# Value columns projected as token rows, keys scaled ahead of queries, and a freed tile for gates, in one hybrid transformer layer

## The chip, the cores and the metric

The kernel runs on one core of one Trainium2 chip. The metric is the device time of one execution in microseconds (us); lower is better. The engines are TensorE (PE; PEld is its weight load), VectorE (DVE), ScalarE (ACT), GpSimd (POOL) and SyncE (SP), which issues most DMAs.

## The reference

One layer on 2048 tokens of width 1024. Only the first of its three sub-layers is touched:

```python
IN_SIZES = (SWA_WIDTH, SWA_KV_WIDTH, SWA_KV_WIDTH,            # 512, 128, 128: window attention
            HGRN_WIDTH, HGRN_WIDTH, HGRN_WIDTH, HGRN_WIDTH)   # 4 x 512: q, f, i (the values), g (the gates)
...
def hgrn2(q, f_logit, i, g, lb, onorm_g):
    """f = lb + (1-lb) sigmoid(f_logit), k = 1-f,
    S_t = diag(f_t) S_{t-1} + k_t i_t^T,  o_t = S_t^T q_t,
    output = RMSNorm(o) * silu(g)."""
    ...
    A = jnp.einsum('bhnqd,bhnkd->bhnqk', qc * jnp.exp(b - b_mid), kc * jnp.exp(b_mid - b))
    A = jnp.where(causal, A, 0.0)
    o_intra = jnp.einsum('bhnqk,bhnkv->bhnqv', A, vc)
    kv = jnp.einsum('bhnkd,bhnkv->bhndv', kc * jnp.exp(b_last - b), vc)
    ...   # scan over chunks of 64: S = decay * S + kv
    o_inter = jnp.einsum('bhnqd,bhndv->bhnqv', qc * jnp.exp(b), S_prev)
    o = (o_intra + o_inter)
    o = rms_norm(o, onorm_g) * jax.nn.silu(g.astype(f32))
```

One input projection, u @ w_in, gives all of q, k, v of the window attention and q, f, i, g of the recurrence (4 heads of 128, chunks of 64 tokens). Behind both stand an output projection, cross attention into 256 memory tokens and a SwiGLU network.

## The kernel before

The sequence is worked in two halves of 1024 tokens. The first half's projection comes first (to about 240 us). Then `in_proj` projects the second half (to about 625 us) while the window attention (`swa_front`, `swa_back`) and recurrence of the first half and, later, the window attention of the second half run between its matmuls. The recurrence of the second half (`hgrn` over pairs 8 to 15; a pair is 128 tokens, two chunks) runs from about 625 to 745 us, between matmuls that fold cross-attention weights together (`fold_cross`, L170 to L172 and L131, L134). From about 765 us on come the big products (L1123 to L1125) to the end.

`in_proj` goes through 22 columns of 128 outputs in the order that `ORDER` lists: per head h the pair (10+h, 6+h), decay and query, then (14+2h, 15+2h); 14 to 17 are the values, 18 to 21 the gates. For a column, `in_cols` loads 1024 x 128 weights (`wcols`), splits them on POOL (L152, whi) and VectorE (L153, wlo), and multiplies them as the stationary operand with the split tokens u, 512 tokens at a time, 24 matmuls for each of two "g" banks (L684, L685, L687). A bank is emptied by ScalarE (L690, tanh, then L697 on VectorE for queries and gates; L704, a copy, for values). So z lies as features by tokens, and is stored to z_d with rows of 1024 tokens. A decay column goes on through `decays`, whose last step is L743 on VectorE. L1033 forms sums of weight tiles for the later products, on VectorE too.

In the recurrence, pair n loads k (`k1`), q (`qq`, `q1`), v and later the gates (`sg`), 512 features by 128 tokens each, from z_d. `hgrn_front`: POOL scales half of q (L868, into qq), TensorE forms the masked products (L878), POOL makes q6 (L884) and scales k (L887), TensorE transposes k and v (L890, L895), ScalarE copies them out (kt at L892, vt at L897). `hgrn_state` updates W from kt and vt (L907, L911 on POOL, L912 on VectorE). `hgrn_out` forms the output from vt, at, W and q6 (L922, L924), with a mean square through POOL (L930 h_vv, L932 h_rs). In the program's names a number ends the tile's own: k18 is k1 of pair 8, q68 is q6 of pair 8, k114 is k1 of pair 14.

The order of the instructions on each engine is not written by hand: the framework schedules the whole program against a simulated timeline, under the limits of the tile rings. io tiles (z, u) have 2 buffers, split weights and raw weights 3, v, kt and sg 1, qq, k1, q6 and vt 2.

Of the kernel before, what the change touches and what calls it, by code (L numbers as in the profile page):

```python
# [23 lines left out]
DFF = 2816  # L24
KT = D // P
NFF = DFF // P
NB = 2
TB = T // NB
NPB = TB // P
# [4 lines left out]
C_KA, C_VA, C_QH, C_FH, C_IH, C_GH = 512, 640, 768, 1280, 1792, 2304  # L34
# [14 lines left out]
class Layer:  # L49
# [125 lines left out]
    def run(self):  # L175
        tc, nc, I = self.tc, self.nc, self.I
        self._n = 0
        kw = dict(reuse_waits="tile")
        self.z_d = tc.dram_tile([DIN, T], F32, name="z_d")
        self.y_d = tc.dram_tile([NT, P, KT, P], F32, name="y_d")  # L180
        self.h1t_d = tc.dram_tile([NT, P, KT, P], F32, name="h1t_d")
        self.pt_d = tc.dram_tile([NT, P, KT, P], F32, name="pt_d")
        self.h1_d = tc.dram_tile([T, D], F32, name="h1_d")
        self.h2_d = tc.dram_tile([T, D], F32, name="h2_d")
        self.qk_d = tc.dram_tile([D, D], F32, name="qk_d")
        self.vo_d = tc.dram_tile([D, D], F32, name="vo_d")
        self.u_d = tc.dram_tile([KT, P, T], F32, name="u_d")
        self.h_d = tc.dram_tile([NFF, P, T], F32, name="hid_d")
        self.y2_d = tc.dram_tile([T, D], F32, name="y2_d")
        with (  # L190
            tc.tile_pool(name="cst", bufs=1) as self.cst,
            tc.tile_pool(name="sm", bufs=3, **kw) as self.sm,
            tc.tile_pool(name="edge", bufs=1, side="right") as edge,
        ):
            self.consts()

            for pool in (self.cst, edge):
                nc.gpsimd.memset(pool.tile([P, 24], F32, name="pad"), 0.0)
# [466 lines left out]
    def in_proj(self, b, u):  # L665
        order = [c for p in self.ORDER for c in p]
        e1 = None
        for cols in [order[:2]] + [[c] for c in order[2:]]:
            e1 = self.in_cols(b, u, cols, e1)
            yield  # L670

    def in_cols(self, b, u, cols, e1):
        nc = self.nc
        w = []
        for c in cols:
            w.append(self.wcols(self.I["w_in"], c))
        z = [self.io_tile("z") for _ in cols]
        for s in range(TB // 512):
            sl = slice(s * 512, (s + 1) * 512)
            for i, c in enumerate(cols):  # L680
                c0 = c * P
                ps = self.bank("g")
                for k in range(KT):
                    nc.tensor.matmul(ps, w[i][0][:, k, :], u[s][k][0], start=(k == 0), stop=False)  # L684
                    nc.tensor.matmul(ps, w[i][0][:, k, :], u[s][k][1], start=False, stop=False)  # L685
                for k in range(KT):
                    nc.tensor.matmul(ps, w[i][1][:, k, :], u[s][k][0], start=False, stop=(k == KT - 1))  # L687
                zs = z[i][:, sl]
                if c0 < C_QH or C_IH <= c0 < C_GH:
                    nc.scalar.activation(zs, ps, AF.Copy)  # L690
                else:
                    nc.scalar.activation(zs, ps, AF.Tanh, scale=0.5)
                    if C_FH <= c0 < C_IH:
                        h = (c0 - C_FH) // P
                        nc.gpsimd.tensor_scalar(zs, zs, self.fb[:, h:h + 1], self.fa[:, h:h + 1], ALU.mult, ALU.add)
                    else:
                        nc.vector.scalar_tensor_tensor(zs, zs, 1.0, ps, ALU.add, ALU.mult)  # L697
# [148 lines left out]
    def hgrn_front(self, n, kinds, f):  # L846
        nc, ph = self.nc, self.hg
        t0 = n * P
        z = self.z_d
        kinds = itertools.cycle(kinds)  # L850

        def get(t, c):
            self.load(t, z[c:c + 512, t0:t0 + P].rearrange("(h p) t -> p h t", p=P))
            return t

        def new(tag, bufs=1, w=P):
            return ph.tile([P, 4, w], F32, tag=tag, name=f"{tag}{n}", bufs=bufs)
# [4 lines left out]
        k1 = get(new("k1", 2), C_FH)  # L862
        qq = new("qq", 2, 192)
        q1 = get(qq[:, :, 0:P], C_QH)
        v = get(new("v"), C_IH)
        g1 = self.G1[:, n, :].unsqueeze(2).broadcast_to([P, 4, 64])

        nc.gpsimd.tensor_tensor(qq[:, :, P:192], qq[:, :, 64:P], g1, ALU.mult)  # L868

        at = self.atz[n % 2]  # L870
        if n < 2:
# [2 lines left out]
        for i in range(2):  # L874
            ps = self.bank(next(kinds))[:, 0:384].rearrange("p (h t) -> p h t", h=2)
            hs = slice(2 * i, 2 * i + 2)
            for r in range(2):
# [2 lines left out]
            nc.scalar.activation(at[0:64, hs, 64:P], ps[0:64, :, P:192], AF.Copy)  # L880

        yield
        q6 = new("q6", 2)
        nc.gpsimd.tensor_tensor(q6.rearrange("p h (c t) -> p h c t", t=64), q1.rearrange("p h (c t) -> p h c t", t=64),  # L884
                                self.G[:, n, :, :].unsqueeze(3).broadcast_to([P, 4, 2, 64]), ALU.mult)

        nc.gpsimd.tensor_tensor(k1[:, :, 0:64], k1[:, :, 0:64], g1, ALU.mult)  # L887
        ps = self.bank(next(kinds))
        for h in range(4):
            nc.tensor.transpose(ps[:, h * P:(h + 1) * P], k1[:, h, :], self.ident)  # L890
        kt = new("kt")
        nc.scalar.activation(kt, ps.rearrange("p (h t) -> p h t", h=4), AF.Copy)  # L892
        ps = self.bank(next(kinds))
        for h in range(4):
            nc.tensor.transpose(ps[:, h * P:(h + 1) * P], v[:, h, :], self.ident)  # L895
# [892 lines left out]
```

## Time and profile before

| | |
|---|---|
| time, median of 3 runs | 2548.94 us (2548.52 to 2550.93) |
| profiled execution | 2549.81 us, span 2548.1 us |
| mean granted TensorE clock | 0.997 |
| TensorE busy | 2508.5 us, 12004 matmul records |
| VectorE, ScalarE, POOL busy | 1761.2, 1250.5, 461.8 us |

In a timeline row stand start, duration, engine, line, operation, output and inputs by the program's names without numbers, stationary and moving shape, and, in brackets, the idle time before it and what ended that. Matmuls overlap, so the distance of their starts is the pace, not the duration. A group row gives the same for all instructions of a kind: count, then busy time and mean ns, then idle time before them.

### The profile page before, as it was taken

To read this page: it belongs to the slowest core of one execution; us is meant where nothing else is said; L and a number is where in the kernel's file an instruction comes from. 1 tells how busy PE (TensorE), PEld (TensorE's weight loads), DVE (VectorE), ACT (ScalarE), POOL (GpSimd) and SP (SyncE) were. 2 spreads that over 40 slices of the span, in tenths; PEclk is the share of its full clock that TensorE was granted. 3 is DMA by queue.
4 is the path that set the end of the run, shared out by engine and by line. 5 is a ranking of instruction groups with operands and counts; after the bars stand their busy time and mean duration, and the time that the engine had idled before them with its cause. 6 is when DMAs were issued, how large, how long until landed. Compare 5 with 4: busy or idle time off the path is not lost. (4 is left out here: it accounts for less than half of the span.)

```text
span 2548.1 us, 34095 instructions
## 1 busy us (share of the span) xinstructions
PE 2508.5 (98%) x12004; PEld 2090.5 (82%) x12004; DVE 1761.2 (69%) x2813; ACT 1250.5 (49%) x2606; POOL 461.8 (18%) x641
## 2 busy tenths in 40 slices
PE   8999999999999999999999999999999999999998
PEld 7777888878998878888788888888888888888886
DVE  6869587788767587787875655586566566664756
ACT  5454366556655566565554333353333344543543
POOL 2233233223412243233210000000000000000022
PEclk9999999999999999999999999999999999999999
DMA  6263544566987795859974542254555433666798
GB/s 240 96 218 137 175 140 139 165 202 209 296 303 223 210 279 196 280 187 253 302 229 133 175 147 79 95 182 144 182 195 194 161 128 132 205 209 195 223 226 207
DMA packets 269386, 489.97 MB, mean 192 GB/s; under 512 B 20640, under 2 KB 127136, under 8 KB 268704
## 3 DMA queue, kind: packets, MB, share of 16 engines
q1 hardware_dynamic: 255392, 438.52, 51.1%
q0 software_dynamic: 12672, 46.14, 9.0%
q10 hardware_dynamic: 1152, 3.15, 0.3%
q8 instruction: 94, 1.54, 0.3%
q14 instruction: 76, 0.62, 0.1%
HBM read 326.26 MB, written 161.48 MB: 191 GB/s over the span
## 5 line engine op out<-in xcount | busy, mean ns | idle before, releaser
L1123 PE MATMUL psm<-T,S 128*128 128x512 f32 x2744 | 1063.5, 392 | 9.5 <-ACT S L986 4.9
L1124 PE MATMUL psm<-T,S 128*128 128x512 f32 x2744 | 1070.8, 390 | 0.0
L1125 PE MATMUL psm<-T,S 128*128 128x512 f32 x2744 | 1063.9, 391 | 3.0 <-DVE S L989 2.5
L1123 PEld LDWEIGHTS psm<-T,S 128*128 128x128 f32 x2744 | 516.0, 188 | 121.6 <-ACT S L986 6.2
L1125 PEld LDWEIGHTS psm<-T,S 128*128 128x128 f32 x2744 | 515.7, 188 | 114.8 <-DVE S L989 7.4
L1124 PEld LDWEIGHTS psm<-T,S 128*128 128x128 f32 x2744 | 516.0, 188 | 106.5
L986 ACT ACTIVATE S<-sum 128x512 fp32r<-128x512 f32 (+1 forms) x336 | 205.9, 618 | 328.5 <-PE psm L1125 325.5
L989 DVE TENSOR_TENSOR S<-sraw,S 128x512 fp32r<-128x512 f32 (+1 forms) x312 | 211.0, 683 | 214.9 <-ACT S L986 193.8
L989 DVE TENSOR_TENSOR S<-sum,S 128x512 fp32r<-128x512 f32 (+1 forms) x400 | 271.9, 685 | 77.8 <-ACT S L986 61.9
L1138 ACT ACTIVATE part<-psm 128x512 f32<-128x512 f32 x294 | 173.2, 592 | 184.4 <-PE psm L1125 183.1
L986 ACT ACTIVATE S<-sraw 128x512 fp32r<-128x512 f32 (+1 forms) x271 | 165.9, 617 | 161.9 <-PE psm L1125 149.5
L1495 POOL DMA_DIRECT2D row<-y_d x28 | 25.0, 891 | 1071.3 <-DMA sraw<-hid_d 905.3
L1466 ACT ACTIVATE junk<-row 128x512 f32<-128x512 f32 x160 | 99.6, 625 | 96.1 <-DVE row L1488 32.6
L684 PE MATMUL psg<-u,whi 128*128 128x512 f32 x352 | 142.5, 405 | 3.7 <-DVE z L697 2.2
L989 DVE TENSOR_TENSOR T<-row,T 128x1024 fp32r<-128x1024 f32 x104 | 124.3, 1202 | 31.7 <-ACT T L986 31.5
L685 PE MATMUL psg<-u,whi 128*128 128x512 f32 x352 | 142.5, 405 | 0.0
L986 ACT ACTIVATE T<-row 128x1024 fp32r<-128x1024 f32 x104 | 105.3, 1023 | 23.3 <-DMA row<-in_w_down_dram 9.8
L687 PE MATMUL psg<-u,wlo 128*128 128x512 f32 x352 | 96.0, 402 | 0.7 <-DVE wlo L153 0.7
L153 DVE TENSOR_TENSOR wlo<-raw,whi 128x1024 fp32r<-128x1024 f32 x54 | 68.3, 1269 | 39.0 <-ACT whi L150 16.4
L1670 DVE TENSOR_TENSOR part<-psm,part 128x512 f32<-128x512 f32 x66 | 45.5, 689 | 63.8 <-PE psm L1125 63.5
L1661 DVE TENSOR_TENSOR row<-psm,part 128x512 f32<-128x512 f32 x66 | 45.5, 689 | 55.3 <-PE psm L1125 52.7
L988 POOL TENSOR_SCALAR S<-sum 128x512 fp32r<-128x512 f32 x64 | 50.8, 795 | 168.9 <-PE psm L1125 136.0
(343 smaller groups left out, 3462.8 us busy)
## 6 DMA issues: line engine op xcount, KB each, us to landing
sraw<-in_w_gate_dram SPq DMA_DIRECT2D x44, 512.0 KB, 5.0
sraw<-in_w_up_dram SPq DMA_DIRECT2D x44, 512.0 KB, 4.9
hid_d<-row SPq DMA_DIRECT2D x44, 512.0 KB, 2.8
h_d<-row SPq DMA_DIRECT2D x32, 512.0 KB, 7.0
y_d<-row SPq DMA_DIRECT2D x32, 512.0 KB, 3.6
sraw<-hid_d SPq DMA_DIRECT2D x32, 512.0 KB, 5.0
row<-h_d POOLq DMA_DIRECT2D x30, 512.0 KB, 7.7
row<-y_d POOLq DMA_DIRECT2D x28, 512.0 KB, 7.6
```

The costliest lines, as they stand in the source:

```text
L153: nc.vector.tensor_tensor(lo, raw, f32(hi), ALU.subtract)
L684: nc.tensor.matmul(ps, w[i][0][:, k, :], u[s][k][0], start=(k == 0), stop=False)
L685: nc.tensor.matmul(ps, w[i][0][:, k, :], u[s][k][1], start=False, stop=False)
L687: nc.tensor.matmul(ps, w[i][1][:, k, :], u[s][k][0], start=False, stop=(k == KT - 1))
L986: self.nc.scalar.activation(hi, raw, AF.Copy)
L988: self.nc.gpsimd.tensor_scalar(hi, raw, 1.0, 1.0, ALU.mult, ALU.mult)
L989: self.nc.vector.tensor_tensor(lo, raw, f32(hi), ALU.subtract)
L1123: nc.tensor.matmul(ps, s[:, 0, k, :], t[:, 0, k, :], start=st, stop=False, **kw)
L1124: nc.tensor.matmul(ps, s[:, 0, k, :], t[:, 1, k, :], start=False, stop=False, **kw)
L1125: nc.tensor.matmul(ps, s[:, 1, k, :], t[:, 0, k, :], start=False, stop=sp, **kw)
L1138: nc.scalar.activation(t, ps, AF.Copy)
L1466: self.nc.scalar.activation(junk, a, AF.Square, scale=float(D) ** -0.5, accum_out=to)
```

## The change

Three things are done for the second half only.

1. The value columns 14 to 17 are computed the other way round: tokens (128 of them) are the stationary operand and 256 value features the moving one (`value_cols`, `in_values`). w_in's value columns come as a host array `w_v` of four blocks, two of them (two raw tiles, two split pairs) for each half of the features. A bank holds two groups of 128 tokens by 256. The result goes to a new DRAM array v_d, tokens by 512 features. Pairs 8 to 15 load `vt` straight from it; their v tile, its four transposes and the copy fall away.
2. k is scaled before q6 is made, and for pairs 8 to 15 `issue_after` keeps q6 of a pair, and the scaled half of q of the next pair, behind the scaled k.
3. The gates of pairs 9, 11, 13, 15 take the buffer of tag "v", which no second-half pair uses now.

```diff
+        self.v_d = tc.dram_tile([TB, 512], F32, name="v_d")
...
         for cols in [order[:2]] + [[c] for c in order[2:]]:
-            e1 = self.in_cols(b, u, cols, e1)
+            c0 = cols[0] * P
+            if not C_IH <= c0 < C_GH:
+                e1 = self.in_cols(b, u, cols, e1)
+            else:
+                i, s = divmod(cols[0] - C_IH // P, 2)
+                if not s:
+                    w = self.value_cols(i)
+                self.in_values(i, s, u, w)
             yield
+
+    def value_cols(self, i):
+        w = []
+        for q in range(2):
+            raw = self.raw_tile()
+            self.load(raw, self.I["w_v"][2 * i + q])
+            hi, lo = self.split_tiles()
+            self.split(raw, hi, lo)
+            hi, lo = (t.rearrange("p (k c) -> p k c", c=256) for t in (hi, lo))
+            w += [(hi[:, k, :], lo[:, k, :]) for k in range(4)]
+        return w
+
+    def in_values(self, i, s, u, w):
+        nc = self.nc
+        z = self.io_tile("z")
+        for q in range(2):
+            ps = self.bank("g")
+            for j in range(2):
+                ts = slice((2 * q + j) * P, (2 * q + j + 1) * P)
+                pr = ps[:, j * 256:(j + 1) * 256]
+                for k in range(KT):
+                    nc.tensor.matmul(pr, u[s][k][0][:, ts], w[k][0], start=(k == 0), stop=False)
+                    nc.tensor.matmul(pr, u[s][k][1][:, ts], w[k][0], start=False, stop=False)
+                for k in range(KT):
+                    nc.tensor.matmul(pr, u[s][k][0][:, ts], w[k][1], start=False, stop=(k == KT - 1))
+            nc.scalar.activation(z[:, q * 512:(q + 1) * 512], ps, AF.Copy)
+        self.store(self.v_d[s * 512:(s + 1) * 512, i * 256:(i + 1) * 256].rearrange("(n p) c -> p n c", p=P),
+                   z.rearrange("p (n c) -> p n c", c=256))
...
-        v = get(new("v"), C_IH)
+        if n < NPB:
+            v = get(new("v"), C_IH)
+        else:
+            vt = new("vt", 2)
+            self.load(vt.rearrange("p h t -> p (h t)"), self.v_d[(n - NPB) * P:(n - NPB + 1) * P, :])
...
-        nc.gpsimd.tensor_tensor(qq[:, :, P:192], qq[:, :, 64:P], g1, ALU.mult)
+        with self.tc.issue_after(self.scaled) if n > NPB else contextlib.nullcontext():
+            nc.gpsimd.tensor_tensor(qq[:, :, P:192], qq[:, :, 64:P], g1, ALU.mult)
...
+        nc.gpsimd.tensor_tensor(k1[:, :, 0:64], k1[:, :, 0:64], g1, ALU.mult)
+        self.scaled = nc.cur_bb.bb.instructions[-1]
         q6 = new("q6", 2)
-        nc.gpsimd.tensor_tensor(q6.rearrange(...), q1.rearrange(...), self.G[...], ALU.mult)
-
-        nc.gpsimd.tensor_tensor(k1[:, :, 0:64], k1[:, :, 0:64], g1, ALU.mult)
+        with self.tc.issue_after(self.scaled) if n >= NPB else contextlib.nullcontext():
+            nc.gpsimd.tensor_tensor(q6.rearrange(...), q1.rearrange(...), self.G[...], ALU.mult)
...
-        ps = self.bank(next(kinds))
-        for h in range(4):
-            nc.tensor.transpose(ps[:, h * P:(h + 1) * P], v[:, h, :], self.ident)
-        vt = new("vt", 2)
-        nc.scalar.activation(vt, ps.rearrange("p (h t) -> p h t", h=4), AF.Copy)
+        if n < NPB:
+            ...   # the same five lines
...
-        sg = ph.tile([P, 4, P], F32, tag="sg", name=f"sg{n}")
+        sg = ph.tile([P, 4, P], F32, tag="v" if n > NPB and n % 2 else "sg", name=f"sg{n}")
...
+    w = np.asarray(inputs["w_in"]).reshape(D, DIN)
+    host["w_v"] = np.ascontiguousarray(w[:, C_IH:C_GH].reshape(2, 4, P, 2, 256).transpose(3, 0, 2, 1, 4)).reshape(4, P, D)
```

The scheduler then puts the instructions in another order from the first value column (about 395 us) to the end of the recurrence; outside of that stretch the order is the same. Lines behind the new functions have other numbers in the kernel after: L131 and L170 to L172 stay, L806 is L842 there, L868 L909, L878 L919, L884 L928, L887 L924, L890 L933, L907 L951, L911 L955, L922 L966, L924 L968, L697 L733, L743 L779, L799 L835, L1033 L1077. Three places follow.

TensorE at the start of the second half's recurrence, before (vt8 and v9 are the value tiles of pairs 8 and 9, L895 the transposes of v, L170 and L171 the folding):

```order
L895 MATMUL pst_855_6500<-ident_77,v8_6463 128x128 x4
L890 MATMUL psg_854_6493<-ident_77,k18_6459 128x128 x4
L878 MATMUL pst_864_6579<-qq9_6569,k19_6567 128x192 x2
L131 MATMUL psh_841_6407<-ident_77,u_836_6392 128x128 x4
L131 MATMUL psh_848_6431<-ident_77,u_843_6416 128x128 x4
L170 MATMUL pss_851_6446<-mT0_6388,whi_850_6442 128x256
L907 MATMUL psg_862_6560<-vt8_6505,kt8_6498 128x128 x4
L878 MATMUL psg_863_6574<-qq9_6569,k19_6567 128x192 x2
L895 MATMUL pst_868_6614<-ident_77,v9_6571 128x128 x4
L922 MATMUL pst_872_6656<-vt8_6505,atz0_2022 128x128
```

The same place after:

```order
L933 MATMUL psg_854_6686<-ident_78,k18_6652 128x128 x4
L131 MATMUL psh_841_6600<-ident_78,u_836_6585 128x128 x4
L919 MATMUL pst_863_6765<-qq9_6755,k19_6753 128x192 x2
L966 MATMUL pst_870_6835<-vt8_6656,atz0_2023 128x128
...
L131 MATMUL psh_848_6624<-ident_78,u_843_6609 128x128 x4
L170 MATMUL pss_851_6639<-mT0_6581,whi_850_6635 128x256
L951 MATMUL psg_861_6746<-vt8_6656,kt8_6691 128x128 x4
L919 MATMUL psg_862_6760<-qq9_6755,k19_6753 128x192 x2
L171 MATMUL pss_851_6639<-mT1_6582,whi_850_6635 128x256
```

The two groups of transposes of v are gone, half of the L131 transposes stands ahead of pair 9's first products (qq9, k19), and pair 8's output stands behind them at once.

POOL at the same place, before (w_se and w_dn belong to the window attention):

```order
L868 TENSOR_TENSOR qq8_6461<-qq8_6461,G1_216 128x4x64
L884 TENSOR_TENSOR q68_6490<-qq8_6461,G_215 128x512
L868 TENSOR_TENSOR qq9_6569<-qq9_6569,G1_216 128x4x64
L884 TENSOR_TENSOR q69_6604<-qq9_6569,G_215 128x512
L806 TENSOR_TENSOR w_se_794_6034<-sink_202,w_mn_790_6012 128x4
...
L887 TENSOR_TENSOR k18_6459<-k18_6459,G1_216 128x4x64
L868 TENSOR_TENSOR qq10_6710<-qq10_6710,G1_216 128x4x64
L887 TENSOR_TENSOR k19_6567<-k19_6567,G1_216 128x4x64
```

And after:

```order
L909 TENSOR_TENSOR qq8_6654<-qq8_6654,G1_217 128x4x64
L842 TENSOR_TENSOR w_se_794_6227<-sink_203,w_mn_790_6206 128x4
...
L924 TENSOR_TENSOR k18_6652<-k18_6652,G1_217 128x4x64
L928 TENSOR_TENSOR q68_6684<-qq8_6654,G_216 128x512
L909 TENSOR_TENSOR qq9_6755<-qq9_6755,G1_217 128x4x64
L974 TENSOR_SCALAR h_vv_872_6850<-h_ss_871_6844 128x4
L976 TENSOR_TENSOR h_rs_873_6852<-h_vv_872_6850,mhalf_83 128x4
L924 TENSOR_TENSOR k19_6753<-k19_6753,G1_217 128x4x64
```

q68 and qq9 moved from ahead of the window attention's last steps to behind k18. At the end of the recurrence k114 (pair 14) moved likewise: before it stands behind qq15, h_vv, h_rs and W14, after ahead of q614, qq15 and W14.

VectorE in the projection, where the bank psg_699 of a query column is emptied, before (z_666 is a decay column, w_mn and S11 are scores of window pair 11):

```order
L799 ISA S11_10_5172,w_mn_683_5170<-pss_685_5173,wmask_2013,nsink_204 128x256
L799 ISA w_mn_683_5170 128x1
...
L799 ISA S11_11_5182,w_mn_683_5170<-pst_686_5183,wmask_2013,nsink_204 128x256
L799 ISA w_mn_683_5170 128x1
L743 SCALAR_TENSOR_TENSOR z_666_5029<-z_666_5029,u_670_5085 128x1024
L1033 TENSOR_TENSOR x_673_5102<-x_673_5102,x_674_5104 128x1024
L697 SCALAR_TENSOR_TENSOR z_698_5261<-z_698_5261,psg_699_5262 128x512
```

And after:

```order
L779 SCALAR_TENSOR_TENSOR z_666_5222<-z_666_5222,u_670_5278 128x1024
L1077 TENSOR_TENSOR x_673_5295<-x_673_5295,x_674_5297 128x1024
L733 SCALAR_TENSOR_TENSOR z_698_5454<-z_698_5454,psg_699_5455 128x512
L879 TENSOR_TENSOR ys9_5164<-psh_663_5208,ys9_5164 64x512
L835 ISA S11_01_5342,w_mn_676_5330<-psh_679_5343,wmask_2014,nsink_205 128x256
...
L835 ISA S11_10_5365,w_mn_683_5363<-pss_685_5366,wmask_2014,nsink_205 128x256
```

The emptying of psg_699, with the decay's step and the sum ahead of it, moved from behind the scores of window pair 11 to ahead of its last three blocks.

More of the change, by code (lines that the diff above doesn't have):

```diff
@@ L688, in in_cols @@
                 zs = z[i][:, sl]
-                if c0 < C_QH or C_IH <= c0 < C_GH:
+                if c0 < C_QH:
                     nc.scalar.activation(zs, ps, AF.Copy)
@@ L882, in hgrn_front @@
         yield
+        nc.gpsimd.tensor_tensor(k1[:, :, 0:64], k1[:, :, 0:64], g1, ALU.mult)
+        self.scaled = nc.cur_bb.bb.instructions[-1]
         q6 = new("q6", 2)
-        nc.gpsimd.tensor_tensor(q6.rearrange("p h (c t) -> p h c t", t=64), q1.rearrange("p h (c t) -> p h c t", t=64),
-                                self.G[:, n, :, :].unsqueeze(3).broadcast_to([P, 4, 2, 64]), ALU.mult)
-        nc.gpsimd.tensor_tensor(k1[:, :, 0:64], k1[:, :, 0:64], g1, ALU.mult)
+        with self.tc.issue_after(self.scaled) if n >= NPB else contextlib.nullcontext():
+            nc.gpsimd.tensor_tensor(q6.rearrange("p h (c t) -> p h c t", t=64),
+                                    q1.rearrange("p h (c t) -> p h c t", t=64),
+                                    self.G[:, n, :, :].unsqueeze(3).broadcast_to([P, 4, 2, 64]), ALU.mult)
         ps = self.bank(next(kinds))
@@ L892, in hgrn_front @@
         nc.scalar.activation(kt, ps.rearrange("p (h t) -> p h t", h=4), AF.Copy)
-        ps = self.bank(next(kinds))
-        for h in range(4):
-            nc.tensor.transpose(ps[:, h * P:(h + 1) * P], v[:, h, :], self.ident)
-        vt = new("vt", 2)
-        nc.scalar.activation(vt, ps.rearrange("p (h t) -> p h t", h=4), AF.Copy)
+        if n < NPB:
+            ps = self.bank(next(kinds))
+            for h in range(4):
+                nc.tensor.transpose(ps[:, h * P:(h + 1) * P], v[:, h, :], self.ident)
+            vt = new("vt", 2)
+            nc.scalar.activation(vt, ps.rearrange("p (h t) -> p h t", h=4), AF.Copy)
         f[n] = q6, at, kt, vt
```

## The prediction, made before the kernel was run

> **What bounds the kernel now.** I read the page first, for the engine that carries the span, then the waits of TensorE between 230 and 800 us, the stretch in which the second half is projected and its recurrence runs, then the rows around each wait.
>
> ```profile
> span 2548.1 us, 34095 instructions
> PE 2508.5 (98%) x12004; PEld 2090.5 (82%) x12004; DVE 1761.2 (69%) x2813; ACT 1250.5 (49%) x2606; POOL 461.8 (18%) x641
> ```
>
> TensorE is busy for 2508.5 of 2548.1 us. The other engines cost time only where TensorE waits for them, so an edit is worth the TensorE rows it removes plus the TensorE waits it ends, less those it makes. The waits of the stretch, in total, count and longest:
>
> ```profile
> PE psg L684 <- DVE z L697: 2.2, 1, 2.2
> PE pst L895 <- DMA v<-z_d: 2.2, 1, 2.2
> ...
> PE psg L890 <- POOL k L887: 1.2, 1, 1.2
> ...
> PE psh L878 <- DVE W L912: 0.9, 1, 0.9
> ...
> PE psh L839 <- DVE ptl L834: 0.5, 1, 0.5
> PE psg L907 <- ACT kt L892: 0.2, 1, 0.2
> ```
>
> Two of these are by name in the way of the change: L895, the transposes of v, goes for these pairs, and L887, the key scaling, is moved. The first, in a projection column, is followed by something its 2.2 us does not contain. TensorE's timeline there:
>
> ```profile
> 528.17 0.66 PE L684 MATMUL psg<-u,whi 128*128 128x512 f32 x1 [2.22 <-DVE z L697]
> ...
> 531.61 0.47 PE L684 MATMUL psg<-u,whi 128*128 128x512 f32 x1
> 531.92 0.39 PE L685 MATMUL psg<-u,whi 128*128 128x512 f32 x1
> ```
>
> The eight matmuls from 528.17 to 531.61 start 0.43 us apart. The stretches of four microseconds around this wait and around the other of 2.2 us show TensorE's granted clock, the third number from the end:
>
> ```profile
> 528.00:532.00 4.00, 3.83 (x10) 3.02 (x11) 4.00 (x9) 0.90 (x2) 0.58 (x2) 0.57 0.92 290
> ...
> 634.00:638.00 4.00, 3.17 (x28) 3.18 (x29) 2.17 (x5) 0.87 (x2) 1.04 (x1) 1.00 0.91 252
> ```
>
> At 0.57 the first wait cost more than itself; after the second the clock stayed at 1.00.
>
> **Part 1, the value matmuls.** 192 matmuls that move 512 columns (4 columns of W, 2 token halves, 24 each) become 384 that move 256. Both paces stand in the trace, as starts of a run of matmuls that wait for nothing; the 256-wide ones belong to the folding and load a new stationary tile each time.
>
> ```profile
> 519.82 0.39 PE L684 MATMUL psg<-u,whi 128*128 128x512 f32 x1
> ...
> 522.62 0.63 PE L687 MATMUL psg<-u,wlo 128*128 128x512 f32 x2
> ...
> 643.83 0.28 PE L170 MATMUL pss<-mT,whi 128*128 128x256 f32 x1
> ...
> 645.25 0.60 PE L890 MATMUL psg<-ident,k 128*128 128x128 f32 x4
> ...
> L1123 PEld LDWEIGHTS psm<-T,S 128*128 128x128 f32 x2744 | 516.0, 188 | 121.6 <-ACT S L986 6.2
> ```
>
> Twelve 512-wide in 2.80 us are 0.2333 each, twelve 256-wide in 1.42 us are 0.1183 each. So 384 x 0.1183 - 192 x 0.2333 = 45.4 - 44.8 = +0.6 us. The reason to doubt it is the weight load: there are 192 more, and the page gives one 188 ns of busy time, more than 118. The 256-wide run shows that such loads already overlap each other and the matmuls, since a pair starts every 118 ns. If they did not here, the pace would be 0.188: 72.2 - 44.8 = +27.4. I take +0.6, the row of the same shape, and keep +27.4 as a rival.
>
> [...]
>
> Copies out of the banks stay two on ScalarE per column; weights keep their bytes and their number of split operations, two whole tiles ahead of a pair of columns rather than one ahead of each. v_d's store and the vt loads take fewer, longer runs than z_d's, off TensorE's path.
>
> **Part 2, the transposes.** Each of the eight second-half pairs loses four transposes of v:
>
> ```profile
> 654.23 0.60 PE L895 MATMUL pst<-ident,v 128*128 128x128 f32 x4
> 654.59 0.37 PE L172 MATMUL psh<-mT,wlo 128*128 128x256 f32 x1
> 654.79 0.28 PE L170 MATMUL psh<-mT,whi 128*128 128x256 f32 x1
> ...
> L895 PE MATMUL pst<-ident,v 128*128 128x128 f32 x32 | 4.9, 276 | 2.2 <-DMA v<-z_d 2.2
> ```
>
> The group takes 0.36 us to the next start, and that matmul needs 0.20 to its successor where 0.118 is usual: 0.44 in all. Eight groups (x32) are -3.5 us. Their eight ScalarE copies go too, at no gain, since TensorE waits for none. The 2.2 us in the group row goes as well if vt8 and vt9 are there: their loads need only v_d, whose last column is stored eight columns before the projection ends, and vt has two buffers, where v9 had to wait for v8's.
>
> **Part 3, the order on POOL and what TensorE finds at the recurrence's start.** These are the rows there, of TensorE and of POOL, and the group row of q on POOL:
>
> ```profile
> 627.87 0.60 PE L895 MATMUL pst<-ident,v 128*128 128x128 f32 x4
> 628.30 0.60 PE L890 MATMUL psg<-ident,k 128*128 128x128 f32 x4
> 628.74 0.82 PE L878 MATMUL pst<-qq,k 128*128 128x192 f32 x4
> 629.39 1.04 PE L131 MATMUL psh<-ident,u 128*128 128x128 f32 x8
> 630.25 0.36 PE L170 MATMUL pss<-mT,whi 128*128 128x256 f32 x1
> ...
> 634.83 0.66 PE L895 MATMUL pst<-ident,v 128*128 128x128 f32 x4 [2.22 <-DMA v<-z_d]
> ...
> 636.80 0.36 PE L171 MATMUL pss<-mT,whi 128*128 128x256 f32 x1
> ...
> 626.73 0.61 POOL L887 TENSOR_TENSOR k<-k,G 128x256 f32<-128x256 f32 x1 [11.88 <-PE pst L878]
> 632.63 0.69 POOL L868 TENSOR_TENSOR qq<-qq,G 128x256 f32<-128x256 f32 x1 [5.29 <-DMA qq<-z_d]
> ...
> 698.54 1.04 POOL L911 TENSOR_TENSOR W<-W,G 128x512 f32<-128x512 f32 x1
> ...
> L884 POOL TENSOR_TENSOR q<-qq,G 128x512 f32<-128x512 f32 x6 | 8.1, 1350 | 15.2 <-PE pst L924 15.2
> ```
>
> Before, q68, qq9 and q69 were done on POOL long ahead of 626.73. Now q68 and qq9 stand behind k18, which waits for the first products of pair 8. k18 ends at 627.34, q68 (1.35) at 628.7, qq9 (0.69) at 629.4. TensorE, without the first L895 group, does k18's transposes at 627.87, half of the L131 group (0.43) and is at pair 9's products at 628.73. That is a new wait of about 0.8 us; with q68 at 1.04 (the W row, of that shape) it is 0.4, with another operation of 1.35 us let in ahead 2.0. Behind TensorE's wait stand pair 8's outputs and the folding; nothing else is late by it. The next thing due is the folding's first long run at L171, whose mT on VectorE does not wait for v: TensorE would reach it at about 636.80 - 2.22 - 0.19 - 0.87 + 0.8 = 634.3.
>
> The third wait, L890 on pair 14's key:
>
> ```profile
> 695.98 0.90 POOL L868 TENSOR_TENSOR qq<-qq,G 128x256 f32<-128x256 f32 x1 [2.51 <-DMA qq<-z_d]
> ...
> 699.55 1.62 POOL L887 TENSOR_TENSOR k<-k,G 128x256 f32<-128x256 f32 x1
> ...
> 701.22 0.66 PE L890 MATMUL psg<-ident,k 128*128 128x128 f32 x4 [1.22 <-POOL k L887]
> ```
>
> Pair 14's key stands behind qq15, which waits 2.51 us for its load, and W14 (the row of 698.54 above). In the new order k114 is ahead of both, so it is ready at least W's 1.04 earlier: -1.0 us of the 1.22. In the pairs between, POOL keeps a gap and k has moved ahead of q, which TensorE needs later; I put those at 0. The kt wait of 0.2 stands behind 628.30 and goes with the extra room (-0.2). The sg tile in v's place lets a gate load start sooner; no TensorE wait names sg, so 0.
>
> Recurrence: -3.5 - 2.2 - 0.2 - 1.0 + 0.8 = -6.1 us; with Part 1's +0.6, -5.5.
>
> **Part 4, the projection stretch from the first value column on, put in a new order.** The wait at 528.17 came out of VectorE's order:
>
> ```profile
> 525.16 1.22 DVE L743 SCALAR_TENSOR_TENSOR z<-z,u 128x1024 f32<-128x1024 f32 x1
> 526.29 1.22 DVE L1033 TENSOR_TENSOR x<-x,x 128x1024 f32<-128x1024 f32 x1
> 527.43 0.68 DVE L697 SCALAR_TENSOR_TENSOR z<-z,psg 128x512 f32<-128x512 f32 x1
> ```
>
> L697 empties the bank that TensorE wants. Ahead of it stood the last step of a decay, a square sum and, before those, the score passes of a window pair. In the new order the decay's step, L1033 and L697 all come ahead of those score passes. An estimate by carrying the durations of before's rows through the new order from the first value column on: the bank comes free 1.8 us before TensorE is back at it. So I expect the wait gone, -2.2, and with it the half-clock stretch, 8 x (0.43 - 0.233) = -1.6.
>
> [...]
>
> The trace of before cannot show the waits that the new order makes. The two small ones of the old order that are listed above and are VectorE's late result are 0.9 (L878) and 0.5 (L839). I take +1.4 for new ones, as much as these two, between 0 and one like 528.17 with its half-clock stretch, 3.8. Total here: -2.2 - 1.6 + 1.4 = -2.4.
>
> **Sum.** -5.5 - 2.4 = -7.9 us. The profiled execution took 2549.81 us (span 2548.1 and 1.7 around it), 0.9 above the median of 2548.94; so 2541.9 by the profile and **2541.0 us** by the median. The measurement tells 0.2% (5.1 us) from no change: faster is below 2543.8, slower above 2554.0.
>
> **Rivals.** *The projection's wait stays or comes back at another bank, half-clock stretch and all.* For it: the 1.8 us of room is an estimate over some 100 us of reordered rows. Against: the rows that made the wait are no longer in that order. It gives -7.9 + 3.8 = -4.1, 2544.8. Chance 0.20, most of it within 0.2%.
>
> *POOL becomes the recurrence's limit*, since qq and q now wait for k in each pair. For it: qq9's 0.8. Against: k waited for TensorE, not POOL, in the earlier pairs, and qq's loads end late anyway. If all seven later pairs wait 0.8: -7.9 + 5.6 = -2.3, 2546.6. Chance 0.07.
>
> *Slower: VectorE stands before the gates' L697 at several decays.* In the new order, too, a decay's step or L1033 (1.22 each) stands right ahead of an L697 at several columns, and the two weight splits of a value pair now follow each other. It needs both g banks full at that moment. Each such stop costs 2.2 + 1.6 = 3.8. Two make -5.5 + 7.6 = +2.1, 2551.0, still within; from three on it is slower: -5.5 + 11.4 = +5.9, 2554.8. Chance 0.10.
>
> *The weight load is not hidden at 256 columns* when it follows value tiles. 384 x 0.188 - 44.8 = +27.4 for +0.6, 2541.0 + 26.8 = 2567.8; it outweighs the rest from 0.139 us a matmul (44.8 + 8.5 over 384). The trace's 0.118 speaks against it. Chance 0.03. [...]
>
> *More than forecast:* no new waits and the 0.8 gone, 2541.0 - 2.2 = 2538.8, or, where a wait outside the stretch falls away too, 2537. Chance 0.06.
>
> **How the numbers follow.** The forecast case keeps 0.54. Faster: nine tenths of that, all of the last case and a third of the first rival, 0.49 + 0.06 + 0.07 = 0.62, given as 0.61. Slower: 0.10 + 0.03 and 0.01 for the forecast's tail, 0.14. Same: 0.25. The range reaches from 2537.0 (last case) to 2552.0 (two stops at decays and one microsecond), which leaves out the three stops and the weight load, and little below.
>
> **What would show it.** Right: no L895 row after 627 us and no wait on v; in four columns the matmuls L700 to L703, 256 wide, at starts 0.118 us apart in place of L720 to L723; a short wait of pair 9's products for POOL near 629; no wait on L733 (old L697) near column 8's decay, and no run at 0.43. Wrong: 256-wide starts over 0.13 us, waits of L720 for VectorE or ScalarE adding to more than 3 us, more than 3 us of waits for POOL between 625 and 760, or a changed time in the phases after 765 us, where nothing was moved.

## The result and the profile after

The change made the kernel faster: 2543.55 us median (2539.73 to 2549.05, 14 runs) against 2549.99 us (2548.52 to 2552.88, 14 runs of before), a ratio of 0.9974 with a 95% interval of 0.9967 to 0.9981. That is -6.4 us; -7.9 had been forecast. The profiled execution of after took 2546.34 us, 2.8 above its median, so its stages are compared here and not its end.

TensorE's timeline gives three points that both kernels have: the first matmul of the second half's projection, pair 8's transposes of k, and the first matmul of the phases. Before (628.30 is shown in the prediction):

```profile
240.37 0.40 PE L684 MATMUL psg<-u,whi 128*128 128x512 f32 x1
...
765.09 0.50 PE L1123 MATMUL psm<-T,S 128*128 128x512 f32 x1 [0.79 <-ACT S L986]
```

After:

```profile
240.56 0.40 PE L720 MATMUL psg<-u,whi 128*128 128x512 f32 x1
...
625.71 0.60 PE L933 MATMUL psg<-ident,k 128*128 128x128 f32 x4
...
759.19 0.50 PE L1167 MATMUL psm<-T,S 128*128 128x512 f32 x1 [0.79 <-ACT S L1030]
```

| stretch | before | after | difference |
|---|---|---|---|
| first projection matmul to pair 8's transposes of k | 387.93 | 385.15 | -2.78 |
| from there to the phases | 136.79 | 133.48 | -3.31 |
| both | 524.72 | 518.63 | -6.09 |

Up to the phases the trace has -6.1, near the -6.4 of the medians. Behind that point, where both kernels run the same 7944 matmuls in the same order, this one execution took 2.4 us longer, nearly all of it in waits of TensorE, so that its span is only 3.5 us shorter (2544.6 against 2548.1).

The waits of TensorE from 600 to 765 us after:

```profile
PE pss L171 <- DVE mT L134: 1.9, 1, 1.9
PE psg L985 <- ACT atz L921: 1.0, 1, 1.0
PE psm L1167 <- ACT S L1030: 0.8, 1, 0.8
PE psg L919 <- DVE sg L986: 0.6, 1, 0.6
...
PE psg L933 <- POOL k L924: 0.2, 1, 0.2
```

And one of before that the prediction does not show, TensorE waiting for a weight split of the folding near the end of the recurrence:

```profile
PE pss L362 <- DVE wlo L153: 0.6, 1, 0.6
```

The waits on v and on this split are gone, and the one on pair 14's k has shrunk from 1.2 to 0.2. In their place stand three that before did not have, 3.5 us together: on mT (L171), on atz (L985) and on the gate step (L919). The wait at the phases' first matmul (L1167) is 0.8 in both kernels. The first of the three, in VectorE's timeline:

```profile
627.26 0.69 DVE L134 TENSOR_TENSOR mT<-pss,mT 128x512 fp32r<-128x512 f32 x1
631.64 1.23 DVE L1077 TENSOR_TENSOR x<-x,x 128x1024 f32<-128x1024 f32 x1 [3.69 <-DMA x<-in_w_out_dram]
632.78 0.68 DVE L134 TENSOR_TENSOR mT<-pss,mT 128x512 fp32r<-128x512 f32 x1
```

L1077, the last sum of output weights, stands between two splits of mT and waits 3.69 us for its load. Before, it stood there too, and waited less:

```profile
631.63 1.23 DVE L1033 TENSOR_TENSOR x<-x,x 128x1024 f32<-128x1024 f32 x1 [1.52 <-DMA x<-in_w_out_dram]
```

The load was issued 2.2 us earlier than before (at 624.09 for 626.25) and took 2.2 us longer (7.5 for 5.4), so that it landed at the same moment. TensorE waited 1.91 us for it. The run own_gate_tile below has the same order without this wait. The second new wait has the same shape on ScalarE, where both atz copies stand behind a T that waits 5.02 us for a load:

```profile
672.98 1.06 ACT L1030 ACTIVATE T<-z 128x1024 fp32r<-128x1024 f32 x1 [5.02 <-DMA z<-in_w_out_dram]
673.94 0.26 ACT L921 ACTIVATE atz<-psg 64x128 f32<-64x128 f32 x1
```

The third has it on VectorE: the gate step (L986) stands behind L341, a step of the folding that waits 1.28 us for a store out of its tile:

```profile
689.88 0.69 DVE L341 TENSOR_TENSOR qs<-x 128x512 f32<-128x512 f32 x1 [1.28 <-DMA qk_s<-qs]
690.49 0.75 DVE L986 SCALAR_TENSOR_TENSOR sg<-psg,onorm,sg 128x512 f32<-128x512 f32 x1
```

### The profile page after: what moved, and what is told of

It is laid out like the page before. It is cut to its first block, busy times and chain, and to the rows that moved or that the text cites. A ratio compares the mean times of both kernels' runs of the same rounds, so it can differ in the third digit from the quotient of the medians.

```text
span 2544.6 us, 34410 instructions
## 1 busy us (share of the span) xinstructions
PE 2504.1 (98%) x12164; PEld 2096.0 (82%) x12164; DVE 1765.3 (69%) x2813; ACT 1247.3 (49%) x2598; POOL 459.0 (18%) x641
## 5 line engine op out<-in xcount | busy, mean ns | idle before, releaser
L1167 PE MATMUL psm<-T,S 128*128 128x512 f32 x2744 | 1063.5, 392 | 9.8 <-ACT S L1030 3.8
L1167 PEld LDWEIGHTS psm<-T,S 128*128 128x128 f32 x2744 | 516.1, 188 | 121.7 <-ACT S L1030 5.2
L1033 DVE TENSOR_TENSOR S<-sraw,S 128x512 fp32r<-128x512 f32 (+1 forms) x312 | 211.1, 684 | 214.7 <-ACT S L1030 193.6
L1033 DVE TENSOR_TENSOR S<-sum,S 128x512 fp32r<-128x512 f32 (+1 forms) x400 | 272.0, 685 | 77.9 <-ACT S L1030 62.8
L1033 DVE TENSOR_TENSOR T<-row,T 128x1024 fp32r<-128x1024 f32 x104 | 125.2, 1211 | 30.6 <-ACT T L1030 30.3
L720 PE MATMUL psg<-u,whi 128*128 128x512 f32 x288 | 115.8, 402 | 1.7 <-ACT z L726 1.3
L721 PE MATMUL psg<-u,whi 128*128 128x512 f32 x288 | 115.5, 401 | 0.0
L723 PE MATMUL psg<-u,wlo 128*128 128x512 f32 x288 | 79.9, 403 | 0.7 <-DVE wlo L153 0.7
```

The costliest lines, as they stand in the source:

```text
L1033: self.nc.vector.tensor_tensor(lo, raw, f32(hi), ALU.subtract)
L1167: nc.tensor.matmul(ps, s[:, 0, k, :], t[:, 0, k, :], start=st, stop=False, **kw)
```

## The experiments

Theory A: the gain is the value path's, partly as removed transposes and a removed wait on v, partly because the new order of the projection has no long wait; POOL's order and the gate tile give little. Rival B: POOL's order carries the recurrence. For the part of the gain that did not come, theory C: the recurrence's stretch is bound by its loads once TensorE is quicker; rival: only the order in which engines and SP's queue take their work. All ratios below are against the kernel before, with 95% intervals. "Pair 8 to phases" is the stretch of 136.79 us (before) and 133.48 us (after) in the table above. Medians rest on several executions, but waits and stretches on one profiled execution of each kernel.

**Value path alone.** From the full change, POOL's old order and the gates' own tile:

```diff
-        with self.tc.issue_after(self.scaled) if n > NPB else contextlib.nullcontext():
-            nc.gpsimd.tensor_tensor(qq[:, :, P:192], qq[:, :, 64:P], g1, ALU.mult)
+        nc.gpsimd.tensor_tensor(qq[:, :, P:192], qq[:, :, 64:P], g1, ALU.mult)
...   # k scaled behind q6 again, q6 held behind nothing
-        sg = ph.tile([P, 4, P], F32, tag="v" if n > NPB and n % 2 else "sg", name=f"sg{n}")
+        sg = ph.tile([P, 4, P], F32, tag="sg", name=f"sg{n}")
```

> Only the token-row values and their straight load; POOL's order of q and k and the gate tile are as before. Theory A (projection order and transposes carry the gain): the last projection matmul ends some 2.2 us earlier than before, as in the full change; the recurrence loses its 32 transposes and the wait on v, but pair 14's transposes keep a wait for POOL's k of about 1.2 us; in all -5 us against before (ratio 0.998). Rival B (the POOL order carries the recurrence's gain): -2.5 us (0.999), with more than 2 us of TensorE waits on k, q or qq.

Measured: 0.9980 (0.9972 to 0.9989), 2545.17 us, -4.7 against its comparison median of 2549.89. Its waits between 240 and 765 us:

```profile
PE pss L171 <- DVE mT L134: 1.9, 2, 1.6
PE psg L930 <- POOL k L927: 1.6, 1, 1.6
PE pss L363 <- DVE wlo L153: 1.5, 1, 1.5
```

No wait for psg behind VectorE's L733 is listed in it, and its last projection matmul stands 2.9 us earlier than before's, both counted from the first (2.3 in the full change): so far it is as A had it. The wait of 1.6 on k is pair 13's and not pair 14's, as A had expected; pair 14's keys wait 0.6 for W on VectorE. B's 0.9990 lies just outside the interval: most of the gain, about three quarters by the medians, comes without POOL's order and the gate tile. The trace is less kind than the median: pair 8 to phases is 135.97 us.

**POOL's order alone**, in the kernel before:

```diff
+        with self.tc.issue_after(self.scaled) if n > NPB else contextlib.nullcontext():
+            nc.gpsimd.tensor_tensor(qq[:, :, P:192], qq[:, :, 64:P], g1, ALU.mult)
-        nc.gpsimd.tensor_tensor(qq[:, :, P:192], qq[:, :, 64:P], g1, ALU.mult)
...   # k scaled ahead of q6, q6 held behind it, for pairs 8 to 15
```

> Only POOL's order: k scaled ahead of q6, q6 and the next qq held behind it for pairs 8 to 15; values as before. A: the projection keeps its order, its 2.2 us wait and its half-clock stretch; in the recurrence the wait on v stays, pair 14's wait on k (1.2) goes, pair 9's products may wait up to 0.8 for qq: -1.0 to +0.5 us against before (ratio 0.9996 to 1.0002). B: -3 us (0.9988).

Measured: 1.0000 (0.9990 to 1.0011), 2549.83 us. The waits:

```profile
PE pst L898 <- DMA v<-z_d: 3.1, 1, 3.1
...
PE psg L893 <- POOL k L884: 0.4, 1, 0.4
```

The projection's wait of 2.2 us on VectorE is still there, as A had it. The wait on pair 14's k falls from 1.2 to 0.4 and the wait on pair 9's v grows from 2.2 to 3.1, and there is a new one of 0.8 at the gate step. This trace is of the kernel's slowest execution, 6.2 us above its median, so these sizes are no prices; by the median POOL's order alone gives nothing. Whether it gives something on top of the value path (-6.4 in place of -4.7) is not shown, since the two intervals overlap.

**All gates in their own tile**, else the full change:

```diff
-        sg = ph.tile([P, 4, P], F32, tag="v" if n > NPB and n % 2 else "sg", name=f"sg{n}")
+        sg = ph.tile([P, 4, P], F32, tag="sg", name=f"sg{n}")
```

> The full change, but all gates in their own tile. A: no gate load was on TensorE's path, so within 0.5 us of the full change: -6 us against before (0.9976), same waits. B': the gates' load behind a single buffer holds up the last step of the pairs, and banks with it: 1 to 2 us slower than the full change, with new waits of TensorE on banks read at the gate step.

Measured: 0.9979 (0.9971 to 0.9988), 2544.16 us, -5.7, not to be told from the full change. The wait at the gate step is 0.2 us (0.6 in the full change), so the mechanism of B' does not show. But A's "same waits" did not hold either: mT waits 0.5 us in all, k 1.3 and a weight split of the folding 1.3, and atz is not in the list; pair 8 to phases is 134.75 us.

That is worth a second look, for in this kernel TensorE, VectorE, ScalarE and POOL take their work in the same order as in the full change up to about 700 us. Only SP issues gate loads at other places, from 633 us on. So nearly up to the first L171 it is a second execution of the same order:

```profile
x<-in_w_out_dram SPq DMA_DIRECT2D x1, 512.0 KB, 5.3
...
630.28 1.23 DVE L1077 TENSOR_TENSOR x<-x,x 128x1024 f32<-128x1024 f32 x1 [1.47 <-DMA x<-in_w_out_dram]
...
632.18 0.41 PE L171 MATMUL pss<-mT,whi 128*128 128x256 f32 x1
...
685.54 0.66 PE L933 MATMUL psg<-ident,k 128*128 128x128 f32 x4 [1.05 <-POOL k L924]
```

The load of the last sum landed 5.3 us after its issue (the first row, a DMA issue with its KB and us to landing), not 7.5, and TensorE came to L171 5.60 us after pair 8's keys without a wait, where the full change came 7.81 us after them. The wait of 1.91 us thus belongs to one execution's load. Why that load took longer is not shown. The 2.2 us did not last, though: by pair 13's keys, with a wait of 1.05 us for them on POOL, this kernel is at 58.96 us from pair 8's and the full change at 59.12.

**The last sum behind mT.** From the full change; the last of its 32 steps runs once the folding's tokens are split:

```diff
-                        for _ in range(4):
+                        for _ in range(4 if i < NT - NPB else 3):
                             next(sums, None)
...
-                for _ in sums:
-                    pass
...
                 next(fold)
+                with self.tc.issue_after(self.mT_done):   # the last L134
+                    for _ in sums:
+                        pass
```

> The full change, with the last sum of output weights on VectorE put behind the splits of the normalised memory (mT), so that its load does not hold them up. A: the 1.9 us wait of the folding's second matmul goes and nothing takes its place in the next 10 us; the phases begin 1.5 to 1.9 us earlier than with the full change: -8 us against before (0.9969). Rival C (the stretch is bound by its loads): the time comes back as a wait for a load or for an engine behind one between 635 and 760 us, and the total stays at -6.4 (0.9975).

Measured: 0.9971 (0.9962 to 0.9980), 2542.32 us, -7.6. Its waits from 600 to 765 us:

```profile
PE psg L987 <- ACT atz L923: 1.5, 2, 1.1
...
PE psg L921 <- DVE sg L988: 0.5, 1, 0.5
...
PE psg L953 <- ACT kt L937: 0.4, 1, 0.4
PE pss L171 <- DVE mT L134: 0.3, 1, 0.3
```

TensorE came to L171 4.78 us after pair 8's k, not 7.81: 1.9 of these 3.0 us are the wait, the rest is work that now stands behind L171. But pair 8 to phases is 132.83 us, only 0.65 shorter than with the full change. The wait on mT is 1.6 us shorter, and about half of that came back, as 0.5 more on atz and 0.4 on kt. The total is on A's side of the middle, the trace on C's; the interval does not separate this kernel from the full change. And the load that this edit goes around landed 5.4 us after its issue here, so that little was to be gained in this execution.

**Fewer loads.** From the full change; the block loaded first is used for all eight blocks of wk_x, wq_x and wv_x. So 21 loads of 512 KB are left out, and seven eighths of these weights with them: the kernel is there for its time alone.

```diff
+            raw = self.raw_tile()
+            self.load(raw, w[0])
             for j in range(KT):
-                wh, wl = self.wcols(w, j, "A")
+                hi, lo = self.split_tiles()
+                self.split(raw, hi, lo, "A")
+                wh, wl = (x.rearrange("p (k c) -> p k c", k=KT) for x in (hi, lo))
...   # the same for wq_x
```

> The full change, with 21 loads of 512 KB left out of the folding: each of wk_x, wq_x and wv_x is loaded for its first block only and that block is used for all eight. Matmuls, splits and their order of need stay. Theory C (the stretch of the second half's recurrence is bound by its loads once the transposes are gone): the waits behind loads (L134's mT 1.9, atz behind a T waiting for its load 1.0, and the one on the gate step 0.6) shrink to under 1 us together, and the time from the recurrence's first transposes of k to the phases falls from 133.5 to about 131 us. Rival A (the waits come from the order in which each engine and SP's queue takes its work): two of the three stay within 0.3 us of their size, and the stretch stays at 133 to 134.

Measured: 0.9954 (0.9940 to 0.9968), 2539.32 us, -11.8. Pair 8 to phases is 130.03 us. All waits of TensorE from 600 to 765 us:

```profile
PE psg L941 <- POOL k L932: 1.1, 1, 1.1
PE psm L1175 <- ACT S L1038: 0.8, 1, 0.8
PE psh L883 <- DVE ptl L878: 0.4, 1, 0.4
PE pss L171 <- DVE mT L134: 0.3, 1, 0.3
```

The load of the last sum landed after 5.2 us here, and in after, by the DMA issues (KB, us from issue to landing):

```profile
x<-in_w_out_dram SPq DMA_DIRECT2D x1, 512.0 KB, 7.5
```

The 21 loads do not explain this difference: with all of them it landed after 5.3 us in own_gate_tile, 5.4 in sum_behind_mT and 5.6 in values_only. The T that stood ahead of the atz copies waited for its load 1.05 us, not 5.02:

```profile
668.12 1.06 ACT L1038 ACTIVATE T<-z 128x1024 fp32r<-128x1024 f32 x1 [1.05 <-DMA z<-in_w_out_dram]
```

The same stretch in the three kernels, by windows from 625 to 765 us (last three numbers: granted clock, DMA share, GB/s), before, after and this one:

```profile
625.00:765.00 140.00, 135.07 (x1043) 128.97 (x1041) 95.69 (x128) 80.81 (x181) 41.63 (x50) 1.00 0.90 298
```
```profile
625.00:765.00 140.00, 135.23 (x1022) 127.97 (x1021) 97.42 (x131) 77.97 (x174) 47.20 (x56) 1.00 0.88 305
```
```profile
625.00:765.00 140.00, 137.72 (x1038) 130.49 (x1037) 99.66 (x132) 79.04 (x176) 48.09 (x56) 1.00 0.75 244
```

Both signs of theory C came: mT, atz and the gate step wait 0.3 us together, in place of 3.5, and the stretch loses 3.45 us. The three waits alone do not decide, since own_gate_tile has only 0.8 us at these places with all its loads. The better evidence is the time to pair 13's keys, up to which TensorE's order is the same in the three kernels. In after and in this kernel they start at

```profile
684.83 0.60 PE L933 MATMUL psg<-ident,k 128*128 128x128 f32 x4
```
```profile
682.76 0.60 PE L941 MATMUL psg<-ident,k 128*128 128x128 f32 x4
```

That is 59.12 us after pair 8's keys in the full change, 58.96 in own_gate_tile and 56.41 here. Two executions with all the loads agree within 0.2 us although their waits differ, and the one with fewer loads is 2.6 to 2.7 us ahead. Over the whole stretch it is the shortest of all kernels, with the least of TensorE's waits (the sum of those listed, with the 0.8 at the phases):

| kernel | pair 8 to phases | TensorE's waits in it |
|---|---|---|
| before | 136.79 | 5.0 |
| after | 133.48 | 4.5 |
| values_only | 135.97 | 7.4 |
| own_gate_tile | 134.75 | 4.5 |
| sum_behind_mT | 132.83 | 3.7 |
| one_fold_load | 130.03 | 2.2 |
| step_1of5 | 133.01 | 3.9 |
| step_3of5 | 134.27 | 4.6 |

So the loads do carry part of the stretch; how much, one execution of each kernel does not settle. Whether it is the bytes in flight or the place in SP's queue that the 21 loads held, this kernel does not separate, since both go with the loads.

**The phase's steps at one place of every pair.** sum_behind_mT, and:

```diff
-                    if i % 4 == 2 and 2 < i < 36:
+                    if i % 5 == 1 and 2 < i < 42:    # step_1of5
+                    if i % 5 == 3 and i < 40:        # step_3of5, the other kernel
```

> The full change with the last sum behind mT as in sum_behind_mT, and the steps that prepare the first phase put at the same place of every pair, behind its first products, in place of every fourth step. Theory A: both atz copies are then ahead of the T that waits for its load on ScalarE, TensorE's waits for atz (1.5 us in sum_behind_mT) go, and the phases begin 1 to 1.5 us earlier than there: -8.5 us against before (0.9967). Theory C: the loads come no earlier, another instruction waits for them: -7.6 (0.997) or the wait for the phases' first T grows from 0.8 to 2 us.

> As step_1of5, with the phase's steps two places later in each pair (behind the transposes of on) and two pairs earlier in all. Theory A: as there, -8.5 us (0.9967), unless the T of the first pairs stands ahead of atz of pair 9 again (then 1 us less). Theory C: -7.6 us (0.997).

Measured: 0.9967 (0.9955 to 0.9980), 2541.06 us, and 0.9969 (0.9958 to 0.9980), 2544.07 us. The first is A's number, the second is nearer C's, and the intervals hold both. Neither trace is A's: pair 8 to phases is 133.01 and 134.27 us, no shorter than in sum_behind_mT. step_1of5 has 0.5 us of atz left, and in its recurrence 1.1 us of waits on k and 1.0 on kt; step_3of5 has one of 3.2 us on atz. As C has it, another instruction waits, though C's other sign, a longer wait of the phases' first matmul, did not come (0.8 in both). Neither is shown to be faster than the full change.

**One sum moved in the kernel before**, to price the projection's wait without the value path:

```diff
-                        for _ in range(4):
+                        for _ in range({2: 3, 3: 5}.get(i, 4)):
                             next(sums, None)
```

> The kernel before, with one sum of output weights (L1033, 1.22 us on VectorE) moved from ahead of the step that empties psg_699 to ten instructions behind it; values, POOL order and gates as before. Theory A (this wait and the half-clock stretch behind it are worth 3.8 us, and the value path gained them by a change of order alone): the 2.2 us wait shrinks to about 1.0 and the clock stays whole there: the last projection matmul 1.2 to 2.8 us earlier than before, and -2.8 us in all (ratio 0.9989). Rival D (a wait of any length there costs a half-clock stretch, or VectorE is late by as much at the next bank): -1 us or nothing (0.9996 to 1.0).

Measured: 0.9992 (0.9983 to 1.0001), 2548.78 us. TensorE at that bank, and its window:

```profile
528.56 0.50 PE L684 MATMUL psg<-u,whi 128*128 128x512 f32 x1 [1.07 <-DVE z L697]
528.89 0.40 PE L685 MATMUL psg<-u,whi 128*128 128x512 f32 x1
529.12 0.40 PE L684 MATMUL psg<-u,whi 128*128 128x512 f32 x1
...
528.00:532.00 4.00, 3.44 (x17) 2.90 (x18) 4.00 (x7) 2.78 (x9) 1.15 (x2) 1.00 0.33 133
```

The wait is 1.07 as expected and the clock stays at 1.00, the matmuls 0.23 apart. The rest of A did not come: the scheduler moved the end of the projection too, and its last matmul stands 3.4 us later than before's, both counted from the first, not 1.2 to 2.8 earlier. The total is not settled: its interval holds both -2 and 0, and the profiled execution, which is 5.1 us above the median, has a new wait of 2.3 us at the recurrence's start. That the wait and the stretch behind it cost 3.8 us at that place is shown by the trace of before; that moving them is worth as much in the total is not.

## Why the prediction was right

The sign and the range held, and the mechanism in the main: the value path's transposes, its wait and the projection's wait went. The sum was 1.5 us too large. It came that near in part by luck, since the projection gave more than forecast and the recurrence less.

**Projection: right, with two terms that missed in opposite directions.** Forecast -1.8 with the matmuls' +0.6; measured -2.34 (-2.78 less 0.44 for the first group of transposes of v, which lies ahead of the second point). L733 no longer keeps TensorE at psg_699, and the granted clock is 1.00 from 240 to 765 us. Of the +1.4 set aside for new waits, 0.4 came:

```profile
596.50 0.50 PE L720 MATMUL psg<-u,whi 128*128 128x512 f32 x1 [0.37 <-DVE z L733]
```

The value matmuls' pace is a little worse than the folding's:

```profile
385.77 0.28 PE L701 MATMUL psg<-whi,u 128*128 128x256 f32 x1
...
386.86 0.28 PE L700 MATMUL psg<-whi,u 128*128 128x256 f32 x1
```

Nine starts in 1.09 us are 0.121, against the 0.1183 taken: 384 x 0.121 - 44.8 = +1.7, not +0.6. That the one term is 1.1 worse and the other 1.0 better is luck. The weight load is hidden at this pace (each is busy for 0.189 us in this stream, and one starts every 0.121), and the rival with 0.188 is out.

**Recurrence: what was to go went, the balance is 2.4 us short.** Forecast -6.1; measured -3.75 (-3.31 and the 0.44). The transposes went. The wait on v went. Pair 14's k gave 1.0, the value taken. The new wait for qq9 was taken at 0.8 and is 0.2:

```profile
624.56 0.62 POOL L924 TENSOR_TENSOR k<-k,G 128x256 f32<-128x256 f32 x1 [13.43 <-PE pst L919]
625.13 1.04 POOL L928 TENSOR_TENSOR q<-qq,G 128x512 f32<-128x512 f32 x1
626.13 0.61 POOL L909 TENSOR_TENSOR qq<-qq,G 128x256 f32<-128x256 f32 x1
...
626.15 0.60 PE L131 MATMUL psh<-ident,u 128*128 128x128 f32 x4
626.80 0.92 PE L919 MATMUL pst<-qq,k 128*128 128x192 f32 x4
```

qq9 ends at 626.74, and TensorE, at 0.43 us for the L131 group, was free at 626.58. q68 took 1.04, the lower of the two rows the prediction had; it used the higher one.

**The term that failed** is the one for new waits in the recurrence: 0.8, for qq9 alone, with the sentence that nothing else is late. Besides qq9's 0.2 the trace has 3.5 us of others, on mT, atz and the gate step. The waits that went come to 4.0: v 2.2, k 1.0, kt 0.2, and 0.6 at the folding's weight split, which the prediction left out. So TensorE's listed waits between the two points fell by 0.55 (from 5.03 to 4.48), where the sum had 2.6; the transposes and all the rest gave 3.2, near the 3.5 of the sum. Of the 2.4 us missing, 2.05 are waits.

As to how, the prediction said that mT on VectorE does not wait for v, so that nothing holds TensorE at L171. TensorE came there as early as that: 5.9 us after pair 8's keys if the wait is taken off, where the forecast has 6.4 (634.3 less 627.87). It then waited for mT, which stood not behind v but behind a sum that waited for a load. L1033 stood among the splits of mT before as well, and waited 1.52 us for x; that row was in the trace of before, and the prediction did not use it. The other two waits have the same shape: the prediction asked which engine's result was late, and not which transfer an engine in between would meet earlier.

The sizes are another matter. own_gate_tile, in the same order, has no wait at the first L171 and none on atz, but others in their place, and the same 4.5 us in all. That such waits are set by the loads fits one_fold_load, which gives back 3.45 us; what would remain of the 2.4 over many executions of the full change is not shown.

**The rivals.** VectorE ahead of L697 at several decays did not come (0.4 us in all), nor POOL as the limit. The projection's wait on VectorE did not come back in after or in the six variants with the value path; the longest of its kind there is 1.0 us (step_3of5).

**The gate tile** at 0: not told from 0.

## What to carry to other kernels

When an edit lets an engine arrive earlier in a stretch where the DMA engines are busy nine tenths of the time (0.90 before and 0.88 after from 625 to 765 us), look, for each engine it then meets, at the next instruction that waits for a transfer, and at what stands behind that instruction in the same queue. In this case a new order moved such waits (3.7 to 7.4 us in six kernels), and only leaving out loads lowered them much (to 2.2).

Before a wait is priced, look for a second execution of the same order. own_gate_tile was one by accident: a wait of 1.91 us that looked like the full change's own was one load's in one execution.

## What the runs showed of the hardware

TensorE's granted clock fell behind some of its long waits. In the four-microsecond windows that hold a wait's end and follow it, it stayed at 1.00 behind waits of 1.07 us (one_sum_later, shown above) and 1.91 us (after, at 633.52). It fell to 0.67 behind 2.00 us in pool_order_only:

```profile
267.87 0.50 PE L684 MATMUL psg<-u,whi 128*128 128x512 f32 x1 [2.00 <-ACT z L690]
...
268.00:272.00 4.00, 4.00 (x13) 3.15 (x14) 2.93 (x3) 0.31 (x1) 0.03 (x1) 0.67 0.41 135
```

It fell as well (in brackets the lowest of these windows) behind 2.22 us at 528.17 (0.57) and 2.92 us at 1252.40 (0.50) of before, 2.59 us at 1247.81 of after (0.50), 2.30 us at 634.24 of one_sum_later (0.78), 3.11 us at 638.24 of pool_order_only (0.75) and 3.24 us at 686.37 of step_3of5 (0.67). Behind three waits of this length it stayed at 1.00: 2.22 us at 634.83 of before, 2.23 us at 1247.25 of step_1of5 and 2.33 us at 1244.26 of step_3of5. In before and after, from 240 us to TensorE's last matmul, no shorter wait was followed by a lower clock. So from 2.00 to 2.33 us a wait went either way; what decides it is not shown.

The lowest clock of a window is 0.50. Counted at that, what the windows lack comes to about 3.4 us behind the wait at 528.17 of before, the one of one_sum_later, the one at 638.24 of pool_order_only and the one of step_3of5, and to 6.8 us behind the waits near 1250 us of before and after. What it costs shows behind the phases' start, where all ten kernels run the same 7944 matmuls in the same order. TensorE is busy there for 1765.6 and 1765.7 us in the two traces with 6.8 us at half clock (before and after), for 1764.5 us in one_sum_later and 1763.5 us in one_fold_load, which have 3.4 us there, and for 1761.4 us in step_1of5, which has none. Before and step_1of5:

```profile
765.09:2548.10 1783.01, 1765.62 (x7944) 1458.72 (x7944) 1182.43 (x1726) 827.65 (x1616) 223.94 (x309) 1.00 0.62 192
```
```profile
760.38:2539.30 1778.92, 1761.41 (x7944) 1457.18 (x7944) 1182.21 (x1726) 827.84 (x1616) 221.21 (x309) 1.00 0.62 192
```

So a stretch of 3.4 us is worth about 2 us, an estimate from these busy times (4.2 us for 6.8), and an execution can gain or lose 2 to 4 us at a place that no edit touched. Differences of that size between single executions are not to be read as the edit's.
